# One more expert weight unit in the ring of a hybrid encoder layer, and the memory it moves into

## Chip, core and metric

The kernel runs on one core of a Trainium2 chip. The metric is device time in microseconds of one execution of the whole layer. The profile is of one execution of the same program; its engines are PE (TensorE matmul), PEld (weight load into TensorE), DVE (VectorE), ACT (ScalarE), POOL (GpSimd) and SP (SyncE, which issues nearly all DMAs).

## What is computed

The layer takes 512 tokens of width 1024. Three token mixers (a 2-D neighbourhood attention, a grouped-query attention and a cross-attention into 256 memory tokens) run on one input projection; their outputs are projected, gated, summed and put through an output matrix. Then a layer norm, a router with expert choice (each of 16 experts takes its 64 best tokens), a SwiGLU expert network, and a second layer norm.

```python
merged = jnp.sum(gates * proj, axis=2)
mix = jnp.einsum('bsd,de->bse', merged, w_out[l])
x = layer_norm(DN_ALPHA * x + mix, ln1_g[l], ln1_b[l])
ffn = expert_choice_ffn(x, w_router[l], w_gate_up[l], w_down[l])
x = layer_norm(DN_ALPHA * x + ffn, ln2_g[l], ln2_b[l])
...
h = jnp.einsum('becd,edf->becf', xs, w_gate_up)
hg, hu = jnp.split(h, 2, axis=-1)
ye = jnp.einsum('becf,efd->becd', jax.nn.silu(hg) * hu, w_down)
```

Everything is float32. The experts' weights are 16 times 12 units of 128 partitions x 2048 numbers, which is 1,048,576 bytes a unit: 8 units of gate and up ("gu") and 4 of down ("dn") for each expert. They are 201 of the 251 MB that the kernel moves.

## The kernel before

The order of work is written out by hand; no scheduler moves it. Each engine runs its instructions in program order, and tiles of a pool that share a tag share memory: a later tile of the tag waits until the earlier one has been read for the last time.

Stages, in order: memory tokens and their keys; queries; the gates and projections of the three branches, with attention units interleaved; `g_na_gates` (eight gate products of branch 0); `g_na_proj` (eight projections of branch 0, numbered j = 0 to 7); the output product (`wo`, then `woc` for the second half of the columns) with the first layer norm and the router's logits mixed in; sorting of the affinities to find each expert's cut; then the 16 experts, and the second layer norm.

**Splitting.** Weights of the dense part come by `Stream` (L149 on): a raw unit is loaded (L167), ACT casts its high part (L97) and DVE subtracts to get the low part (L98); a product is three matmuls of high and low parts. The raw buffer has two halves, so a load waits for the DVE of two units before.

**`g_na_proj` (L961 to L980).** For each j: 12 matmuls into a PSUM bank of the tag `mm` (three banks in turn); then on DVE L971 (gate times product, which empties the bank), L972 (add the sum so far); on ACT L973 (the high part `mh`); on DVE L980 (the low part `ml`), one j later. Every second j a unit is split: ACT L97, DVE L98. `run(gen)` (L803 on) takes one background function from the list `bg` after every piece; that is how small work is put between.

**Router preparation (L920 to L950).** `rt` is a tile in the memory tag `bf` that holds small arrays: the scaled router weights `wg_t`, their sums, statistics, counts. `router_scale` (two products and two reductions on DVE, L938 and L939), `router_sums` (one matmul, L943) and `router_centre` (two DVE operations, L946 and L947) are in `bg` while `g_na_gates` runs.

**The ring of expert units.** `RING` names 12 places in memory (tags); ten hold two units, `raw` and `VS` hold one: 22 units in the first round. `_blocks` gives the order in which units of the sequence 0 to 191 go to places: in the first round one DMA brings a whole place; in the second, up to unit 35, one DMA brings one unit. Three places drop out after one or two rounds. `Ring.load` (L822 on) issues one DMA on SP's queue; `Ring.done` is called when the matmuls of a unit have been emitted and issues every load whose place is then free, so each load waits on SP for the PE's last read of that place. The first four places load during `g_na_gates` and `g_na_proj`, two more at the end of the dense units, `Q6` and `raw` by `ring.upto(8)` in the output product, and `Q9`, `VS`, `G1`, `M` (7 units) by `ring.upto(len(RING))` after it, since those hold arrays of the output product until it ends.

**Other homes.** `gb` (15 x 1024) holds the rows of both layer norms; they are loaded early into `ropesq` (L872), cast by ACT (L877) and corrected by two DVE operations (L881, L884). `r_transpose` puts transposed tokens in two buffers of the tag `tmp`; `a01` and `a23`, the arrays that are sorted, are in two buffers of the tag `t`. In the expert part `hT` and `GT` share the two `tmp` buffers and `GTe` takes `bf`.

**An expert (loop at the end of `layer_kernel`).** `gate_up` (L1312) for the first four units, `h_transpose` of the expert before, `down` of the expert before (L1347), then the other four units; `act_h` (ACT L1322, DVE L1323 and L1324); `slots_T` (L1367) for each pair of experts, `combine` for a finished pair, `gather` after every fourth expert (L1272, L1274) and in pieces during the first two.

Of the kernel before, what the change touches and what calls it, by code (L numbers as in the profile page):

```python
# [9 lines left out]
F32 = mybir.dt.float32  # L10
# [30 lines left out]
def lead(e):  # L41
    return 2 if e == NEXP - 2 else 4


def _blocks():
    order = []
    for e in range(NEXP - 1):
        order += [("gu", e, k) for k in range(lead(e))]
        if e:
            order += [("dn", e - 1, k) for k in range(4)]  # L50
        order += [("gu", e, k) for k in range(lead(e), KD)]
    order += [("gu", NEXP - 1, k) for k in range(KD)]
    order += [("dn", e, k) for e in (NEXP - 2, NEXP - 1) for k in range(4)]
    blocks, i, r = [], 0, 0
    while i < len(order):
        for tag, n in RING:
            left = ROUNDS.get(tag, len(order)) - r
            if left > 0 and i < len(order):
                keys = order[i:i + n]
                i += n  # L60
                if r and (i < FULL or i > len(order) - N_SINGLE):
                    blocks += [(tag, h, [key]) for h, key in enumerate(keys)]
                else:
                    blocks.append((tag, 0, keys))
        r += 1
    return blocks
# [3 lines left out]
def layer_kernel(ctx: ExitStack, tc: tile.TileContext, xt, xn, first0, wu, bgate, rpb, gains, wrt,  # L70
# [193 lines left out]
    nc.sync.dma_start(lnT[:, :2], lnt)  # L264
    gb = cp.tile([15, D], F32R, name="gb")
    gb_s, gb_c, gb_t = (cp.tile([15, n], F32, name="gb_" + k)[:, :1] for k, n in (("s", 1), ("c", 1), ("t", 33)))
# [185 lines left out]
    def g_gqa():  # L452
# [23 lines left out]
        a, b = rope[1:]  # L476
        bg.extend([lambda: None, a[4], b[0], a[5], b[1], b[2], b[3], norm_hi, b[4], b[5]])

# [335 lines left out]
    class Ring:  # L814
# [52 lines left out]

    norm_raw = []

    def load_norms():  # L870
        norm_raw.append(vs_t[:15, 1])
        nc.sync.dma_start(norm_raw[0], lnp)  # L872

    after[14] = [load_norms]

    def norm_hi():
        nc.scalar.copy(gb, norm_raw[0])  # L877

    def norm_mask():
        norm_raw.append(vs_t[:15, 0])  # L880
        nc.vector.tensor_scalar(norm_raw[1], gb.bitcast(F32), gb_c, None, op0=ALU.mult)  # L881

    def norm_lo():
        nc.vector.scalar_tensor_tensor(gb, norm_raw[0], gb_s, norm_raw[1], op0=ALU.mult, op1=ALU.add)  # L884


# [32 lines left out]

    rt = R("bf", [P, 12, 64], "rt")  # L920
    aff = rt[:, 0].rearrange("p (m e) -> p m e", m=NT)
    cnt = rt[:, 2:4].rearrange("p a (m e) -> p m a e", m=NT)
    st_all = rt[:, 5:7].rearrange("p a b -> p (a b)")[:, :96].rearrange("p (m q s) -> p m q s", m=NT, q=4)
    ones_f = rt[:, 7:9].rearrange("p a b -> p (a b)")
    nc.gpsimd.memset(ones_f, 1.0)
    lgA = rt[:, 9].rearrange("p (m e) -> p m e", m=NT)
    rb = rt[:, 10][:, :NEXP]
    wsum = rt[:, 10][:, NEXP:3 * NEXP].rearrange("p (a e) -> p a e", a=2)
# [3 lines left out]
    wg_t = rt[:, 2:4].rearrange("p a (k e) -> p (a k) e", e=NEXP)  # L932
    wb_t = rt[:, 0:2].rearrange("p a (k e) -> p (a k) e", e=NEXP)
    wps = []
# [18 lines left out]
    dump("ynh", ST["y0"][0].bitcast(F32))  # L953
    dump("macc", ST["macc"])

# [25 lines left out]

    tri_t = [rt[:, 4].bitcast(F16), rt[:, 11].bitcast(F16), tri_d]
    for i in range(3):
# [12 lines left out]
    a01 = R("t", [48, P], "a01", bufs=2)  # L996
    a23 = R("t", [48, 64 + P], "a23", bufs=2)
    nc.gpsimd.memset(a01, 0.0)
    nc.gpsimd.memset(a23, 0.0)
    top = cp.tile([48, 64], F32, name="top")  # L1000
# [125 lines left out]
    us += ws.take(2)  # L1126
    ring.upto(8)

# [76 lines left out]
    keep_warm(28)  # L1205
    ring.upto(len(RING))
    dump("aff", aff)
# [95 lines left out]
    def gate_up(e, ks):  # L1303
# [3 lines left out]
        for k in ks:  # L1307
            w = ring.get("gu", e, k)
            xs = XS[qd][k // 4][:, k % 4, i * CAP:(i + 1) * CAP]
            for b in range(2):  # L1310
                for hf in range(2):
                    nc.tensor.matmul(GU[e][b][hf * 64:hf * 64 + 64], xs,  # L1312
                                     w[b][:, hf * 512:hf * 512 + 512],
                                     start=(k == 0), stop=(k == KD - 1))
# [11 lines left out]
    def h_transpose(e, tp=None):  # L1326
# [4 lines left out]
        if e == 0:  # L1331
            homes.extend((R("tmp", [P, 4, P], "hT", bufs=2), R("tmp", [P, NT, P], "GT", F32R, bufs=2)))
        t = R("bf", [P, 4, P], f"hT{e}") if e == NEXP - 1 else homes[0]
# [29 lines left out]
    def slots_T(pr):  # L1363
        qd, h = divmod(pr, 2)
        gp = PB("mm", f"gT{pr}", (P, NT, P))
        for m in range(NT):
            nc.tensor.matmul(gp[:, m], OH[qd][:, m, h * P:(h + 1) * P], id16, start=True, stop=True)  # L1367
        if pr == 0:
            homes.append(R("bf", [P, NT, P], "GTe", F32R))
        g = homes[1 if pr % 2 else 2]  # L1370
        GT[pr] = g
# [4 lines left out]
    def acc_of(m):  # L1376
# [3 lines left out]
        return ACC[m // 2][:, m % 2]  # L1380

    def ln_row(row, h, nm):
        bc = PB("mm", nm)
        nc.tensor.matmul(bc, gsel[:, row:row + 1].to_broadcast([15, P]), gb[:, h * 512:h * 512 + 512], start=True, stop=True)
        return bc
# [60 lines left out]
    def last_down(g2, xq, spare):  # L1446
# [118 lines left out]
        def low_rank(m, h):  # L1565
            nc.tensor.matmul(tl[m, h], rows[:13, m * P:(m + 1) * P], gb[:13, h * 512:h * 512 + 512], start=bool(h), stop=True)

# [20 lines left out]
    g1 = gather(0, 2, 2)  # L1588
    side = iter(())
    for e in range(NEXP):  # L1590
        if e == 0:
# [4 lines left out]
        elif e < NEXP - 1:  # L1596
# [207 lines left out]
```

## Time and profile before

| | us |
|---|---|
| median of 3 runs | 966.16 (965.75 to 966.56) |
| the profiled execution, its own time | 966.82 |
| its span in the profile | 965.0 |
| PE busy in it | 942.6 (98%) |
| DVE busy | 453.4 (47%) |
| ACT busy | 276.5 (29%) |
| POOL busy | 84.2 (9%) |

The span is the time between the first and the last instruction, and all places in time below are microseconds from its start. 1.8 us of the profiled execution lie around its span. The granted TensorE clock is 0.997 of full speed over the execution. A matmul's end is modelled, and matmuls overlap, so "PE busy" does not say that PE is at its peak.

### The profile page before, as it was taken

Reading aid. Unit: us, or ns where it says so; the run is one execution under the profiler, and the core shown is the slowest. Engines: PE = TensorE matmul, PEld = TensorE weight load, DVE = VectorE, ACT = ScalarE, POOL = GpSimd, SP = SyncE. Lnnn points to the kernel's source line nnn. Section 1 sums busy time; section 2 is a strip of 40 time slices with the busy share of each in tenths; the row PEclk is TensorE's granted clock in tenths of the full one; section 3 lists DMA queues with packets and bytes.
Section 4 is the critical chain, followed back from the end, with each engine's and each line's share of the span. In section 5 each row is a group of like instructions: output and inputs, shape, how many; then the busy total and the mean of one; then the engine's idle time right before and its main releaser. Section 6 shows DMA issues by size and latency. Waiting matters only on the chain.

```text
span 965.0 us, 12910 instructions
## 1 busy us (share of the span) xinstructions
PE 942.6 (98%) x5262; PEld 608.4 (63%) x5262; DVE 453.4 (47%) x851; ACT 276.5 (29%) x539; POOL 84.2 (9%) x98
## 2 busy tenths in 40 slices
PE   9999999999999999999999999999999999998996
PEld 9899878888888888887885333433344333432344
DVE  6347668874376566237454122653322223231426
ACT  6334454543444454223242111100010000100123
POOL 0002303000112231000023000000000000000003
PEclk9999999999999999999999999999999999999998
DMA  9311111111433322564919999999999999999992
GB/s 361 114 67 67 66 66 44 66 58 54 115 91 106 99 83 87 218 266 192 393 43 387 430 418 431 428 432 429 431 429 431 430 431 431 430 430 432 427 410 91
DMA packets 39192, 251.17 MB, mean 260 GB/s; under 512 B 13007, under 2 KB 13391, under 8 KB 24926
## 3 DMA queue, kind: packets, MB, share of 16 engines
q1 hardware_dynamic: 38414, 249.74, 63.8%
q8 instruction: 41, 0.67, 0.3%
q10 hardware_dynamic: 720, 0.62, 0.2%
q14 instruction: 17, 0.14, 0.0%
HBM read 247.46 MB, written 2.10 MB: 259 GB/s over the span
## 4 chain that ended last, share of the span: by engine, by line
PE 79%; DMA 10%; DVE 6%; ACT 2%; issue 2%; POOL 1%; ACTq 0%; DVEq 0%; POOLq 0%; SPq 0%
DMA w<-in_wx 10%; PE g L1312 10%; PE u L1312 9%; PE y L1347 8%; PE gate L282 4%; PE gate L284 4%; PE gate L283 4%; PE gy L670 2%; PE ga L1272 2%; PE pr L282 2%; PE nqk L284 2%; PE nqk L282 2%; PE nqk L283 2%; PE gt L657 1%; PE pr L283 1%
## 5 line engine op out<-in xcount | busy, mean ns | idle before, releaser
L1312 PE MATMUL g<-w,xs 128*64 128x512 f32 x512 | 135.0, 606 | 2.9 <-DMA w<-in_wx 2.9
L1312 PE MATMUL u<-w,xs 128*64 128x512 f32 x512 | 131.6, 592 | 0.0
L1347 PE MATMUL y<-w,hT 128*64 128x512 f32 x480 | 106.6, 594 | 3.3 <-DMA w<-in_wx 2.6
L98 DVE TENSOR_TENSOR y<-y,y 64x512 fp32r<-64x512 f32 x30 | 20.7, 689 | 134.4 <-ACT y L97 134.4
L1312 PEld LDWEIGHTS u<-w,xs 128*64 128x64 f32 x512 | 36.8, 137 | 73.1 <-issue 72.3
L97 ACT CAST y<-y 64x512 fp32r<-64x512 f32 x30 | 17.4, 580 | 224.8 <-PE y L1347 213.5
L98 DVE TENSOR_TENSOR los<-raw_twin,whi 128x1024 fp32r<-128x1024 f32 x42 | 53.4, 1272 | 58.2 <-ACT whi L97 58.0
L1347 PEld LDWEIGHTS y<-w,hT 128*64 128x64 f32 x480 | 33.8, 137 | 72.0 <-issue 64.7
L284 PE MATMUL gate<-xh,los 128*128 128x512 f32 x192 | 74.8, 390 | 0.0
L1312 PEld LDWEIGHTS g<-w,xs 128*64 128x64 f32 x512 | 30.7, 136 | 53.9 <-issue 44.8
L282 PE MATMUL gate<-xh,whi 128*128 128x512 f32 x144 | 57.2, 397 | 0.0
L283 PE MATMUL gate<-xl,whi 128*128 128x512 f32 x144 | 56.1, 390 | 0.0
L1419 DVE TENSOR_TENSOR acc<-acc,cb 128x512 f32<-128x512 f32 x56 | 35.6, 684 | 37.8 <-PE cb L1417 37.8
L97 ACT CAST whi<-raw_twin 128x1024 fp32r<-128x1024 f32 x42 | 44.0, 1049 | 8.2 <-PE wo L1110 4.3
L1488 POOL TENSOR_TENSOR acc<-acc,ln2g 128x512 f32<-128x512 f32 x6 | 7.6, 1276 | 430.1 <-DVE l2s L1516 428.1
L284 PEld LDWEIGHTS gate<-xh,los 128*128 128x128 f32 x192 | 36.0, 188 | 7.7
L98 DVE TENSOR_TENSOR los<-raw_twin,los 128x1024 fp32r<-128x1024 f32 x20 | 25.0, 1249 | 27.0 <-ACT los L97 26.9
L646 ACT ACTIVATE att_twin<-gs,nm 128x512 f32<-128x512 f32 x32 | 21.7, 684 | 49.0 <-DVE nm L645 49.0
L1322 ACT ACTIVATE tg<-g 128x512 f32<-128x512 f32 x16 | 9.5, 597 | 89.2 <-PE g L1312 89.2
L1335 DVE COPY hT<-ht 128x512 f32<-128x512 f32 x15 | 10.4, 691 | 44.4 <-PE ht L1330 44.4
L282 PEld LDWEIGHTS gate<-xh,whi 128*128 128x128 f32 x144 | 27.0, 188 | 6.5 <-issue 1.2
L283 PEld LDWEIGHTS gate<-xl,whi 128*128 128x128 f32 x144 | 27.1, 188 | 5.3
(436 smaller groups left out, 1863.5 us busy)
## 6 DMA issues: line engine op xcount, KB each, us to landing
w<-in_wx SPq DMA_DIRECT2D x83, 2048.0 KB
raw_twin<-in_wu SPq DMA_DIRECT2D x65, 512.0 KB
w<-in_wx SPq DMA_DIRECT2D x26, 1024.0 KB
raw<-in_wu SPq DMA_DIRECT2D x8, 512.0 KB
xr<-in_xt SPq DMA_DIRECT2D x4, 512.0 KB
macc<-in_xn SPq DMA_DIRECT2D x2, 1024.0 KB
first<-in_first SPq DMA_DIRECT2D x4, 384.0 KB
bf<-in_rpb SPq DMA_DIRECT2D x64, 24.0 KB
```

The costliest lines, as they stand in the source:

```text
L97: nc.scalar.copy(hi, src)
L98: nc.vector.tensor_tensor(lo, src, hi.bitcast(F32), op=ALU.subtract)
L282: nc.tensor.matmul(acc, w_h, rh[:, k], start=(k == 0), stop=False)
L283: nc.tensor.matmul(acc, w_h, rl[:, k], start=False, stop=False)
L284: nc.tensor.matmul(acc, w_l, rh[:, k], start=False, stop=(k == nk - 1))
L646: nc.scalar.activation(self.p[:, h], self.s[h], AF.Exp, bias=nm[:, h:h + 1], accum_out=self.sm[:, h:h + 1])
L670: nc.tensor.matmul(self.y[h * 64:h * 64 + 64, :P], ST["vg"][:, kc, kvh * 64:kvh * 64 + 64], self.pt[:, h, kc], start=(kc == 0), stop=(kc = ...
L1272: nc.tensor.matmul(g, XH[:, m, c], oh[:, m, sl], start=(m == 0), stop=False)
L1312: nc.tensor.matmul(GU[e][b][hf * 64:hf * 64 + 64], xs, w[b][:, hf * 512:hf * 512 + 512], start=(k == 0), stop=(k == KD - 1))
L1335: nc.vector.tensor_copy(t, tp)
L1347: nc.tensor.matmul(y[o * 64:o * 64 + 64], hT[:, c, hf * 64:hf * 64 + 64], w[j][:, o * 512:(o + 1) * 512], start=(k == 0 and j == 0), stop= ...
L1419: nc.vector.tensor_tensor(a, a, cb, op=ALU.add)
```

## The change

A thirteenth entry "X" is put into the first round of the ring, right behind `raw`. It holds unit 22 (expert 2, gate and up, k = 2) and is used once. It lies in three pieces: the up half in the tag `gb` (4 KB a partition), the two quarters of the gate half in `bf` and in one buffer of `tmp` (2 KB each). Three DMAs bring it. So the second round begins with unit 23 in place of 22.

The memory comes from here: the norm rows are no longer kept from the start; `norm_rows` loads them in two halves (15 x 512) during experts 2 and 3 into `gb`, after X is used, with three DVE operations each. The router's arrays leave `bf` for two tiles of the tag `t`, so they are set up after `g_na_gates`, and the `bg` list with `router_scale`, `router_sums` and `router_centre` now runs during `g_na_proj`; the affinities get a tile of their own. The sorted arrays are parts of the second tile. One of the two buffers of the transposed tokens goes to the tag `oh`. `slots_T(0)` moves from expert 1 to expert 2. Empty functions keep the other entries of `bg` where they were.

```diff
 def _blocks():
+        if r == 0:
+            blocks.insert([t for t, _, _ in blocks].index("raw") + 1, ("X", 0, order[i:i + 1]))
+            i += 1
         r += 1
...
 class Ring:  # load
+            if tag == "X":
+                key, = keys
+                g = [R("bf", [P, 512], "wxa"), R("tmp", [P, 512], "wxb", bufs=2)]
+                u = R("gb", [P, D], "wxc")
+                nc.sync.dma_start(u, src[:, 1])
+                nc.sync.dma_start(g[1], src[:, 0, 512:])
+                nc.sync.dma_start(g[0], src[:, 0, :512])
+                self.t[key] = [g, u]
+                self.at[key] = (tag, 0)
+                self.row += P
+                self.n += 1
+                return
...
-    after[14] = [load_norms]
-    def norm_hi():
-        nc.scalar.copy(gb, norm_raw[0])
...
-    bg.extend([norm_mask, norm_lo])
+    bg.extend([lambda: None, lambda: None])
...
-    rt = R("bf", [P, 12, 64], "rt")
-    aff = rt[:, 0].rearrange("p (m e) -> p m e", m=NT)
...
+    run(g_na_gates(), 1.0)
+    at.drain()
...
+    rt, rt1 = (R("t", [P, 8, 64], n, bufs=2) for n in ("rt", "rt1"))
+    aff = cp.tile([P, NT, NEXP], F32, name="aff")
...
+    a01 = rt1[:48, 2:4].rearrange("p a b -> p (a b)")
+    a23 = rt1[:48, 4:7].rearrange("p a b -> p (a b)")
...
     bg.extend([lambda: None, router_scale, lambda: None, router_sums, router_centre])
-    run(g_na_gates(), 1.0)
-    at.drain()
...
+    x1T = [R("tmp", [P, 4, P], "x1T", bufs=2), R("oh", [P, 4, P], "x1To")]
     def r_transpose(m, k0, n=4):
-        t = R("tmp", [P, n, P], f"x1T{m}{k0}", bufs=2)
+        x1T.append(x1T.pop(0))
+        t = x1T[0][:, :n]
...
-    ring.upto(8)
+    ring.upto(9)
...
-    ring.upto(len(RING))
+    ring.upto(len(RING) + 1)
...
+    def norm_rows():
+        GB.append(R("gb", [15, D], "gb", F32R))
+        for h in range(2):
+            c = slice(h * 512, h * 512 + 512)
+            raw = R("t", [15, 512], f"nraw{h}", bufs=2)
+            nc.sync.dma_start(raw, lnp[:, c])
+            yield
+            part = R("t", [15, 512], f"npart{h}", bufs=2)
+            nc.vector.tensor_copy(GB[0][:, c], raw)
+            nc.vector.tensor_scalar(part, GB[0][:, c].bitcast(F32), gb_c, None, op0=ALU.mult)
+            nc.vector.scalar_tensor_tensor(GB[0][:, c], raw, gb_s, part, op0=ALU.mult, op1=ALU.add)
+            yield
...
                 if k == lead(e) - 1:
                     h_transpose(e - 1)
+                    if e in (2, 3):
+                        steps(nrm)
...
-            if e % 2:
-                slots_T(e // 2)
+            if e % 2 and e > 1 or e == 2:
+                slots_T((e - 1) // 2)
...
             for k in range(lead(e), KD):
+                if e in (2, 3) and k == KD - 1:
+                    steps(nrm)
                 gate_up(e, (k,))
```

More of the change, by code (lines that the diff above doesn't have):

```diff
@@ L476, in g_gqa @@
         a, b = rope[1:]
-        bg.extend([lambda: None, a[4], b[0], a[5], b[1], b[2], b[3], norm_hi, b[4], b[5]])
+        bg.extend([lambda: None, a[4], b[0], a[5], b[1], b[2], b[3], lambda: None, b[4], b[5]])
     def g_na_v():
@@ L866, in layer_kernel @@
     vs_t = R("VS", [P, 2, 1024], "ropesq")
[L868 to L872, printed above, removed]
-    after[14] = [load_norms]
-    def norm_hi():
-        nc.scalar.copy(gb, norm_raw[0])
[L879 to L884, printed above, removed]
     run(g_mem())
@@ L918, in layer_kernel @@
     run(g_branch(1, False, between), 0.5)
-    rt = R("bf", [P, 12, 64], "rt")
-    aff = rt[:, 0].rearrange("p (m e) -> p m e", m=NT)
-    cnt = rt[:, 2:4].rearrange("p a (m e) -> p m a e", m=NT)
-    st_all = rt[:, 5:7].rearrange("p a b -> p (a b)")[:, :96].rearrange("p (m q s) -> p m q s", m=NT, q=4)
-    ones_f = rt[:, 7:9].rearrange("p a b -> p (a b)")
-    nc.gpsimd.memset(ones_f, 1.0)
-    lgA = rt[:, 9].rearrange("p (m e) -> p m e", m=NT)
-    rb = rt[:, 10][:, :NEXP]
-    wsum = rt[:, 10][:, NEXP:3 * NEXP].rearrange("p (a e) -> p a e", a=2)
+    run(g_na_gates(), 1.0)
+    at.drain()
+    dump("ynh", ST["y0"][0].bitcast(F32))
+    dump("macc", ST["macc"])
+    rt, rt1 = (R("t", [P, 8, 64], n, bufs=2) for n in ("rt", "rt1"))
+    aff = cp.tile([P, NT, NEXP], F32, name="aff")
+    cnt = rt[:, 0:2].rearrange("p a (m e) -> p m a e", m=NT)
+    st_all = rt[:, 4:6].rearrange("p a b -> p (a b)")[:, :96].rearrange("p (m q s) -> p m q s", m=NT, q=4)
+    ones_f = rt[:, 6:8].rearrange("p a b -> p (a b)")
+    nc.gpsimd.memset(ones_f, 1.0)
+    lgA = rt1[:, 0].rearrange("p (m e) -> p m e", m=NT)
+    rb = rt1[:, 1][:, :NEXP]
+    wsum = rt1[:, 1][:, NEXP:3 * NEXP].rearrange("p (a e) -> p a e", a=2)
+    a01 = rt1[:48, 2:4].rearrange("p a b -> p (a b)")
+    a23 = rt1[:48, 4:7].rearrange("p a b -> p (a b)")
+    nc.gpsimd.memset(a01, 0.0)
+    nc.gpsimd.memset(a23, 0.0)
     tri_d = cp.tile([P, P], F16, name="tri_d")
@@ L931, in layer_kernel @@
     nc.gpsimd.memset(ones_h, 1.0)
-    wg_t = rt[:, 2:4].rearrange("p a (k e) -> p (a k) e", e=NEXP)
-    wb_t = rt[:, 0:2].rearrange("p a (k e) -> p (a k) e", e=NEXP)
+    wg_t = rt[:, 0:2].rearrange("p a (k e) -> p (a k) e", e=NEXP)
+    wb_t = rt[:, 4:6].rearrange("p a (k e) -> p (a k) e", e=NEXP)
     wps = []
@@ L1331, in h_transpose @@
         if e == 0:
-            homes.extend((R("tmp", [P, 4, P], "hT", bufs=2), R("tmp", [P, NT, P], "GT", F32R, bufs=2)))
+            homes.append(R("tmp", [P, 4, P], "hT", bufs=2))
         t = R("bf", [P, 4, P], f"hT{e}") if e == NEXP - 1 else homes[0]
@@ L1367, in slots_T @@
             nc.tensor.matmul(gp[:, m], OH[qd][:, m, h * P:(h + 1) * P], id16, start=True, stop=True)
-        if pr == 0:
-            homes.append(R("bf", [P, NT, P], "GTe", F32R))
-        g = homes[1 if pr % 2 else 2]
+        if pr < 2:
+            homes.append(R("tmp", [P, NT, P], "GT", F32R, bufs=2) if pr else R("bf", [P, NT, P], "GTe", F32R))
+        g = homes[1 + pr % 2]
         GT[pr] = g
@@ L1380, in acc_of @@
         return ACC[m // 2][:, m % 2]
+    GB = []
+    def norm_rows():
[10 more added lines that the diff above has]
+            yield
     def ln_row(row, h, nm):
         bc = PB("mm", nm)
-        nc.tensor.matmul(bc, gsel[:, row:row + 1].to_broadcast([15, P]), gb[:, h * 512:h * 512 + 512], start=True, stop=True)
+        nc.tensor.matmul(bc, gsel[:, row:row + 1].to_broadcast([15, P]), GB[0][:, h * 512:h * 512 + 512], start=True, stop=True)
         return bc
@@ L1565, in low_rank @@
         def low_rank(m, h):
-            nc.tensor.matmul(tl[m, h], rows[:13, m * P:(m + 1) * P], gb[:13, h * 512:h * 512 + 512], start=bool(h), stop=True)
+            nc.tensor.matmul(tl[m, h], rows[:13, m * P:(m + 1) * P], GB[0][:13, h * 512:h * 512 + 512], start=bool(h), stop=True)
         def finish(m, h):
@@ L1589, in layer_kernel @@
     side = iter(())
+    nrm = norm_rows()
     for e in range(NEXP):
```

11 lines of the change are left out of this document (2 added, 9 removed).

## The prediction, made before the changed kernel ran

> **What bounds the kernel now.** I read the page first: the row of transfer rates by slices, since the change concerns transfers.
>
> ```profile
> GB/s 361 114 67 67 66 66 44 66 58 54 115 91 106 99 83 87 218 266 192 393 43 387 430 418 431 428 432 429 431 429 431 430 431 431 430 430 432 427 410 91
> ```
>
> A slice is 24.1 us. From slice 22 to 38, the whole expert part, the rate stands at 427 to 432 GB/s: the queue is full and stays full. Before that lies slice 20 (482 to 506 us) with 43 GB/s, the pause. At 430 GB/s a unit of 1,048,576 bytes takes 2.44 us. Next the chain of waits from its end backwards (start, duration, what), to see whether that rate sets the end:
>
> ```profile
> 842.93 33.97 DMA w<-in_wx
> ...
> 915.86 19.56 DMA w<-in_wx
> ...
> 935.55 1.98 PE yq L1467 x32
> ```
>
> From 843 us to the first of the last four product parts at 935.55 the chain is transfers alone. A transfer issued at 842.93 needs 34 us to land because of those queued before it, so the expert part ends when its bytes have come, plus a fixed tail of PE and DVE work. Then busy time by stretches (PE, PEld, DVE, ACT, POOL, clock, DMA share, GB/s):
>
> ```profile
> 428.00:452.00 24.00, 22.76 (x99) 18.22 (x98) 20.01 (x28) 8.38 (x13) 0.00 (x0) 1.00 0.53 208
> 452.00:503.00 51.00, 50.72 (x294) 43.86 (x294) 25.79 (x67) 15.83 (x30) 3.68 (x14) 1.00 0.54 212
> 484.00:500.00 16.00, 16.00 (x104) 14.30 (x103) 8.66 (x38) 4.36 (x10) 2.94 (x11) 1.00 0.00 1
> 502.00:570.00 68.00, 66.19 (x450) 32.47 (x449) 22.83 (x83) 15.77 (x30) 11.51 (x12) 1.00 0.97 394
> 502.00:574.00 72.00, 70.19 (x468) 33.82 (x469) 23.52 (x84) 15.77 (x30) 11.51 (x12) 1.00 0.97 396
> 502.00:591.00 89.00, 87.19 (x547) 39.42 (x547) 26.34 (x88) 17.53 (x33) 11.51 (x12) 1.00 0.98 403
> 860.00:940.00 80.00, 73.75 (x374) 26.90 (x372) 20.75 (x34) 11.67 (x21) 0.00 (x0) 1.00 1.00 426
> ```
>
> Between 860 and 940 us PE is idle for 6.25 of 80 us: it has caught up with the transfers and waits for them. That 6.25 us is also all that PE can lose in the expert part before it takes over as the bound. The start of the stream is in SP's waits (us in total, times, longest):
>
> ```profile
> SPq L829 <- PE woc L1109: 25.7, 1, 25.7
> ```
>
> SP waits 25.7 us for the output product to let go of `Q9`'s memory, until 502.9. So the stream starts when PE gets there, and between 452 and 503 PE idles 0.28 of 51 us: what makes PE late at 452 makes the stream, and the end, equally late.
>
> **The unit in the pause: -2.44 us.** X stands on SP's queue behind `raw` and before `Q9`. Its memory is free by then (norm rows gone, `bf` last read by the position bias, `tmp` by the last low part). The transfers end at about 483 us and the stretch from 484 to 500 us moved 1 GB/s, so 2.44 us of transfer, and more than that, are covered by 16 idle us. From 502.9 on, the same places are freed by the same PE work as before, each filled by the unit one further on, and the stream is one unit shorter. This counts in full as long as the queue doesn't run dry where the extra unit is spent. In the third filling of `Q2` (units 44 and 45 in place of 43 and 44) the load must wait for unit 24 and no longer 23.
>
> ```profile
> 502.90 65.34 SPq L829 DMA_DIRECT2D w<-in_wx  x21
> ```
>
> and, in the chain of waits:
>
> ```profile
> 572.04 6.87 PE y L1347 x32
> ```
>
> Those 21 loads, issued by 568.2, are 7 units of the first round, 12 single ones and 9 more in five loads, in all 28. Moved by 574 are 72 us x 396 GB/s = 28.5 MB = 27.2 units (the load that followed at 572 stands behind these). Unit 24 is the first quarter of the product at 572.04, done at 573.8; 0.8 unit, 2.0 us of transfer, is then still queued. `slots_T(0)`, gone from expert 1, lets it be some 0.4 us earlier. So the queue is thin there, but not dry. Price if it is: at most the delay itself, 6.87 / 4 = 1.72 us.
>
> By the Trainium skill (DMA: Bandwidth & Descriptors, Specifications) a core's share of HBM is about 358 GB/s, which would make the unit worth an estimated 2.93 us and the sum below 0.49 us better; the rows at 430 GB/s decide against it.
>
> **The router's preparation, moved from the gates to the projections: +1.59 us.** Six DVE operations move. Their rows, four then two:
>
> ```profile
> 391.95 0.28 DVE L938 TENSOR_TENSOR rt<-wr_t,lnT 128x128 f32<-128x128 f32 x1
> ...
> 393.18 1.22 DVE L98 TENSOR_TENSOR los<-raw_twin,los 128x1024 fp32r<-128x1024 f32 x1
> ...
> 405.10 0.17 DVE L946 COPY rt<-wps 128x16 f32<-128x16 f32 x1
> 405.18 0.28 DVE L947 SCALAR_TENSOR_TENSOR rt<-wps,rt 128x128 f32<-128x128 f32 x1
> ```
>
> The four hold DVE from 391.95 to 393.18, 1.23 us; the two from 405.10 to 405.46, 0.36 us. Where they were, DVE waited between splits, so they cost nothing. Where they go, it does not (DVE, then ACT):
>
> ```profile
> 428.19 1.23 DVE L98 TENSOR_TENSOR los<-raw_twin,los 128x1024 fp32r<-128x1024 f32 x1 [6.42 <-ACT los L97]
> 429.34 0.68 DVE L971 SCALAR_TENSOR_TENSOR tm<-sg,pr 128x512 f32<-128x512 f32 x1
> 430.05 0.69 DVE L972 TENSOR_TENSOR tm<-tm,macc 128x512 f32<-128x512 f32 x1
> 430.66 0.68 DVE L971 SCALAR_TENSOR_TENSOR tm<-sg,pr 128x512 f32<-128x512 f32 x1
> 431.37 0.69 DVE L972 TENSOR_TENSOR tm<-tm,macc 128x512 f32<-128x512 f32 x1
> 431.98 0.69 DVE L980 SCALAR_TENSOR_TENSOR ml<-tm,mh 128x512 fp32r<-128x512 f32 x1
> 433.71 1.23 DVE L98 TENSOR_TENSOR los<-raw_twin,whi 128x1024 fp32r<-128x1024 f32 x1 [1.04 <-ACT whi L97]
> ```
>
> ```profile
> 432.10 0.63 ACT L973 ACTIVATE mh<-tm 128x512 fp32r<-128x512 f32 x1 [0.69 <-DVE tm L972]
> 432.64 1.04 ACT L97 CAST whi<-raw_twin 128x1024 fp32r<-128x1024 f32 x1
> ```
>
> DVE's only pause here is 1.04 us, and it is DVE's own doing: the cast it waits for stands on ACT behind the `mh` copy, which waits for L972. So DVE and ACT form one closed chain, 20.01 us of DVE work in 24, and at its end PE waits for it:
>
> ```profile
> PE wo L1108 <- DVE tm L971: 1.2, 2, 0.8
> ```
>
> ```profile
> 450.32 0.50 PE L1108 MATMUL wo<-whi,mh 128*128 128x512 f32 x1 [0.45 <-DVE tm L971]
> ```
>
> `router_scale` now stands ahead of L971 of j = 1, `router_centre` ahead of L971 of j = 4. Both push every later L971, `mh`, cast and split by their whole length; queued behind them are the emptying of a PSUM bank and ACT's casts, and PE waits for the bank of j = 7 at 450.32. That start moves by 1.23 + 0.36 = 1.59 us. `router_sums` takes one of the three `mm` banks between j = 3 and 4, so PE stands earlier (at j = 4 until L971 of j = 2, at j = 6 until `router_centre`), but these stalls end before the chain does. Bounds: 0, if DVE takes the six in its waits; 2.0, with another 0.4 for PE's restarts at the borrowed bank. I take 1.59: each row of the chain starts as the one before it ends.
>
> **The matmul of `router_sums`, out of the gates: -0.22 us.** PE is never idle there, so its place shows in the steps:
>
> ```profile
> 402.10 0.30 PE L943 MATMUL wps<-rt 128*128 128x32 f32 x2
> 402.24 0.48 PE L282 MATMUL gate<-xh,los 128*128 128x512 f32 x1
> 402.55 0.40 PE L283 MATMUL gate<-xl,los 128*128 128x512 f32 x1
> ```
>
> L283 would follow 0.23 us after 402.10; it starts 0.22 us later than that. In `g_na_proj` the matmul falls into PE's new waits.
>
> **The norm rows: +0.14 us.** Two loads of 30 KB inside the full stream, 61 KB at 430 GB/s. Their six DVE operations (an estimated 1.4 us a half, from half of the old row below and its two companions) lie in DVE's waits in experts 2 and 3, at 26.34 us busy of 89. Removing the old cast and two corrections gains nothing: PE has no wait near them.
>
> ```profile
> L884 DVE SCALAR_TENSOR_TENSOR gb<-ropesq,gb_s x1: 1264/1264/1264, 193.2 to 193.2; 15x1024 fp32r<-15x1024 f32 x1
> ```
>
> ```profile
> 606.78 0.60 ACT L1322 ACTIVATE tg<-g 128x512 f32<-128x512 f32 x1 [3.97 <-PE g L1312]
> ```
>
> ```profile
> 502.90 86.68 SPq L829 DMA_DIRECT2D w<-in_wx  x27
> ```
>
> The second half is the delicate one: its DVE operations stand ahead of expert 3's `act_h`, whose ACT step, at 606.78, must wait for them (it reuses the buffer). It is issued behind the 27th load (the last row, one unit later than there), at about 591 us. By then 28 + 6 x 2 = 40 units are issued and 89 x 403 = 35.9 MB, 34.2 units, moved: 5.8 units, 14.1 us, are ahead of it. It lands near 605, is worked off by 607, and PE loses at most some tenths, out of its 6.25 us.
>
> Homes of transposes, sorted arrays, `hT` and `GT`: as many buffers as before, same instructions, nothing.
>
> **Sum:** -2.44 + 1.59 - 0.22 + 0.14 = -0.93 us. On the profiled execution's 966.82 (span 965.0 and 1.8 around it) that is 965.9; it lies 0.66 above the median, so I expect a median of **965.2**.
>
> **The rivals.**
> - *The six operations cost nothing* (bound 0). For: DVE is idle 17% of 428 to 452. Against: the closed chain. 966.16 - 2.44 - 0.22 + 0.14 = 963.6.
> - *The queue runs dry where X is spent.* For: 2.0 us of reserve only. Against: it is positive, and later loads come every 3.4 us for 4.9 us of transfer. 965.2 + 1.72 = 966.9.
> - *The norm rows land late*, and DVE, ACT and then PE stand behind them; PE becomes the bound and the kernel slower. PE can lose 6.25 - 1.37 - 0.93 = 3.95 us, and three free PSUM banks of `gather` give some 2.6 more; so it decides from a landing at about 612. For: the 34 us of the chain's first row; by it the rows land at 625, 13 us past that point: 978. Against: 5.8 units queued, not 14. By the Trainium skill (DMA: Bandwidth & Descriptors, Queues, rings and completion order) an engine takes descriptors in ring order, so nothing lets the small load pass; the 34 us row agrees.
>
> **How the numbers follow.** Chances: forecast 0.58, free operations 0.20, dry queue 0.12, late rows 0.10. About 0.2%, 1.93 us, is what a measurement of this kernel can tell from no change: faster is below 964.23, slower above 968.09. Faster: all of the second case and 0.06 of the forecast's spread, 0.26. Slower: the late rows, 0.02 of the forecast, 0.02 of the dry queue with DVE's upper bound, 0.14. Within: 0.60. The range goes from the free operations (963.6, less 0.3 for a queue better fed in expert 1) to the dry queue plus 0.4 at the banks, 963.3 to 967.4, and leaves out the late rows and edges. The forecast's own is 964.4 to 966.2.
>
> **What would show it.** X's three loads near 478 to 480 us and next to nothing moved from 488 on; the wait of `wo` on L971 ending near 451.7 and the stream's first load near 504.3, both 1.4 late; no rate below 380 GB/s around 574 to 580; the end of the transfers 0.9 earlier than before; PE's waits for them in the last 80 us shrinking from 6.2 to about 4. Wrong it is if `wo` starts on time, if the rate dips at 575, or if ACT waits for DVE at expert 3.

## The result: 967.4 us, a fifth of a per cent slower

| | before | after |
|---|---|---|
| median, 21 runs each, us | 965.84 (965.04 to 968.42) | 967.40 (965.88 to 972.14) |
| ratio, 95% interval | | 1.0021 (1.0014 to 1.0029) |
| executions above 968.5 us | 0 of 21 | 5 of 21, three of them at 972.0 to 972.1 |
| the profiled execution, its span | 966.82, 965.0 | 972.00, 970.2 |

The forecast was 965.2 with a range up to 967.4: wrong in sign, with the median on the range's upper end. The profiled execution of after is one of the three long ones, so a second profile of the same kernel, of an execution of 966.51 us (span 964.7), is read beside it. It is called the repeat.

First the transfer rates by slices (24 us each) of the page, the long execution, then the repeat:

```profile
GB/s 359 112 66 66 66 66 54 56 74 36 127 112 74 95 84 85 261 268 178 394 94 381 429 420 388 372 416 430 431 429 430 431 430 432 430 431 432 427 399 92
```

```profile
GB/s 358 115 67 67 66 66 48 62 68 44 115 116 82 98 83 88 230 278 169 400 78 384 429 426 433 398 418 428 430 432 428 431 431 429 431 431 431 428 406 92
```

Before, slices 23 to 27 stood at 418 to 432 GB/s. The long execution has 388, 372 and 416 in slices 24 to 26, the repeat 398 and 418 in 25 and 26. Elsewhere in the expert part the rates are those of before. Now stretches of the long execution (columns as in the prediction):

```profile
484.00:500.00 16.00, 16.00 (x104) 14.26 (x103) 8.63 (x37) 4.16 (x10) 2.82 (x11) 1.00 0.10 40
502.00:574.00 72.00, 70.19 (x468) 34.03 (x469) 23.71 (x84) 15.37 (x29) 11.49 (x12) 1.00 0.97 398
574.00:600.00 26.00, 26.00 (x126) 8.65 (x122) 5.13 (x8) 2.34 (x4) 0.00 (x0) 1.00 1.01 394
600.00:640.00 40.00, 35.61 (x196) 15.84 (x194) 20.80 (x36) 5.64 (x10) 0.00 (x0) 0.96 1.00 377
640.00:700.00 60.00, 60.00 (x266) 22.50 (x264) 24.86 (x36) 4.10 (x7) 0.00 (x0) 1.00 1.01 431
860.00:940.00 80.00, 74.83 (x340) 25.54 (x336) 21.33 (x34) 10.26 (x18) 0.00 (x0) 1.00 1.01 429
```

and of the repeat:

```profile
574.00:600.00 26.00, 26.00 (x126) 8.53 (x122) 5.13 (x8) 2.34 (x4) 0.00 (x0) 1.00 1.01 430
600.00:640.00 40.00, 38.59 (x216) 16.69 (x216) 25.31 (x40) 6.26 (x11) 0.00 (x0) 1.00 0.98 402
612.00:636.00 24.00, 23.24 (x128) 9.74 (x129) 15.10 (x24) 2.29 (x4) 0.00 (x0) 1.00 0.97 389
```

X's transfer ends by 488 us, in the pause, as meant. After that, 574 to 640 us is where time is lost: against 430 GB/s the long execution loses 26 x (1 - 394/430) + 40 x (1 - 377/430) = 7.1 us, the repeat 40 x (1 - 402/430) = 2.6 us. The long one moves less with its DMA engines just as busy (share 1.00 to 1.01), the repeat with a share of 0.97 to 0.98. That is the first sign of two different losses. The third thing in this stretch is the norm rows' second half, in the chain of waits of the long execution:

```profile
591.60 19.65 DMA nraw<-in_lnp
...
611.27 0.43 DVE gb L1391
...
612.24 0.75 DVE gb L1393
...
613.06 0.04 ACT tg L1321
...
614.16 1.01 PE ga L1271 x4
```

and on ACT in both executions, the long one first:

```profile
613.06 0.60 ACT L1321 ACTIVATE tg<-g 128x512 f32<-128x512 f32 x1 [10.04 <-DVE gb L1393]
```

```profile
609.24 0.60 ACT L1321 ACTIVATE tg<-g 128x512 f32<-128x512 f32 x1 [6.51 <-DVE gb L1393]
```

The load needed 19.65 us (the repeat: 16.1). ACT's step of expert 3 stood at 606.78 before and behind PE; now it stands behind the rows. PE is busy 35.61 and 38.59 of the 40 us, against 39.25 before. The clock of 0.96 in the long execution is one stretch at half the clock, from 614.0 to 617.4 us, which begins at the end of a wait of PE for ACT, 3.64 us long:

```profile
614.00:617.40 3.40, 3.24 (x16) 2.25 (x16) 2.03 (x4) 0.67 (x2) 0.00 (x0) 0.50 0.98 337
```

It adds to PE's delay here, but an execution can be long without it: the long execution with the rows on ACT's queue, below, has a clock of 1.00 throughout these 40 us.

### The profile page after: what moved, and what is told of

Same layout as the page of the kernel before. It is cut to its first block, busy times and chain, and to the rows that moved or that the text cites. A ratio compares the mean times of both kernels' runs of the same rounds, so it can differ in the third digit from the quotient of the medians.

```text
span 970.2 us, 12928 instructions
## 1 busy us (share of the span) xinstructions
PE 944.1 (97%) x5262; PEld 608.8 (63%) x5262; DVE 454.7 (47%) x855; ACT 275.4 (28%) x538; POOL 84.6 (9%) x98
## 4 chain that ended last, share of the span: by engine, by line
PE 80%; DMA 8%; DVE 6%; ACT 2%; issue 2%; POOL 1%; ACTq 0%; DVEq 0%; SPq 0%; POOLq 0%
PE g L1311 10%; PE u L1311 9%; PE y L1346 9%; DMA w<-in_wx 6%; PE gate L284 4%; PE gate L285 4%; PE gate L286 4%; DMA nraw<-in_lnp 2%; PE gy L672 2%; PE ga L1271 2%; PE pr L284 2%; PE cb L1430 2%; PE nqk L285 1%; PE nqk L286 1%; PE nqk L284 1%
```

## Experiments

Medians in us; the ratio is to the kernel before in runs on the same chip, with its 95% interval. The ratio weighs every execution, so long ones lift it above the quotient of the two medians (rows on ACT's queue: 1.0019 against 1.0006). "Above" counts executions above 968.5, which are called long.

| kernel | median (range) | before | ratio | above |
|---|---|---|---|---|
| the changed kernel again | 967.61 (965.82 to 974.11) | 965.91 | 1.0024 (1.0010 to 1.0038) | 3 of 12 |
| rows on ACT's queue | 966.50 (965.22 to 973.53) | 965.91 | 1.0019 (1.0002 to 1.0036) | 4 of 12 |
| no rows | 966.20 (964.97 to 967.09) | 965.91 | 1.0001 (0.9993 to 1.0010) | 0 of 11 |
| no X | 967.31 (966.70 to 971.67) | 965.91 | 1.0023 (1.0013 to 1.0034) | 3 of 11 |
| 16 rows, ACT's queue | 968.27 (965.95 to 971.36) | 965.80 | 1.0021 (1.0009 to 1.0033) | 5 of 11 |
| no rows, single loads | 964.86 (964.29 to 966.37) | 965.80 | 0.9986 (0.9978 to 0.9995) | 0 of 11 |
| 16 rows, single loads | 967.36 (964.31 to 972.32) | 965.80 | 1.0015 (1.0001 to 1.0028) | 2 of 11 |
| 16 rows, single loads, POOL | 967.25 (963.62 to 972.18) | 965.80 | 1.0014 (0.9996 to 1.0032) | 4 of 12 |
| before, single loads | 966.17 (964.31 to 966.96) | 965.64 | 1.0003 (0.9994 to 1.0011) | 0 of 11 |
| rows in expert 4, single loads, POOL | 965.31 (963.66 to 966.74) | 965.64 | 0.9997 (0.9988 to 1.0006) | 0 of 11 |
| rows in expert 4, POOL | 964.44 (963.38 to 967.10) | 965.64 | 0.9987 (0.9978 to 0.9996) | 0 of 11 |
| rows in expert 4 | 966.00 (965.02 to 966.98) | 965.95 | 1.0001 (0.9992 to 1.0010) | 0 of 11 |
| no X, no rows | 966.77 (965.65 to 967.57) | 965.95 | 1.0006 (0.9997 to 1.0015) | 0 of 11 |

### Are late rows the cause, or slower transfers?

The changed kernel again:

> The changed kernel, unaltered, beside a new set of runs of the one before. If the fall of the transfer rate to 383 GB/s between 576 and 640 us and the second half of the norm rows landing at 611 us belong to every execution, both show in this profile and the time is about 967.4, 1.5 above the kernel before. If they belong only to the executions at 972, this profile shows at least 420 GB/s between 576 and 640, ACT waits for DVE at expert 3 for less than 2 us, and the 1.5 us lie somewhere else.

Neither branch came whole: 430 GB/s up to 600 us, then 402, ACT behind DVE for 6.5 us, and a median of 967.61. Then the loads on a queue of their own:

```diff
-            nc.sync.dma_start(raw, lnp[:, c])
+            nc.scalar.dma_start(raw, lnp[:, c])
```

> The two loads of the norm rows are issued by ACT, on a queue of their own, in place of SP. Theory A (late rows: the second half lands some 20 us after its issue because it stands behind the weights, DVE waits for it 6.8 us, ACT 10 us, PE 3.6 us, and loads are freed later): the second half lands within 5 us of its issue, DVE's and ACT's waits are gone and the kernel falls by 2 to 6 us, to 962 to 965.2, below the kernel before. Theory B (the transfers themselves run slower between 576 and 640 us, whatever DVE does): the waits go but the rate stays near 385 to 400 GB/s and the time stays within 0.7 us of the changed kernel, 966.7 to 968.

The second half is issued at 587.3 and its last packet starts at 591.7, and ACT's wait at expert 3 is 3.97 us behind PE, as before the change. By the Trainium skill (DMA: Bandwidth & Descriptors, Queues, rings and completion order) a DMA engine takes turns between the queues that have work for it; 4.4 us here against 16.1 and 19.65 on SP's queue agrees. The common executions fall to 965.2 to 967.3, with a median of 965.94, where the common ones of the changed kernel's second set had 967.45. The 962 to 965.2 of theory A did not come: 4 of 12 are at 968.9 to 973.5, and the profiled one, at 968.9, has the low rate with full DMA engines:

```profile
574.00:600.00 26.00, 26.00 (x126) 8.65 (x122) 5.13 (x8) 2.34 (x4) 0.00 (x0) 1.00 1.01 386
```

So late rows cost some 1.5 us in the common executions, and are not all of it. No rows at all:

```diff
-            nc.sync.dma_start(raw, lnp[:, c])
+            nc.gpsimd.memset(raw, 1.0)
```

> The norm rows are not loaded at all; POOL fills their two buffers with ones and the six DVE operations work on these (the norm rows are left out of the result's second layer norm and residual). Theory A (late rows): as with a queue of their own, 962 to 965.2. Theory B (slower transfers): 966.7 to 968. Should the small packets of the rows (30 of 2 KB) themselves bring the 16 DMA engines out of step and slow the transfers, this kernel alone is back at 430 GB/s between 576 and 640 us and is some 2 to 6 us faster than the one with a queue of their own.

966.20 with no long execution; none of the three expected times. The rows cost 967.61 - 966.20 = 1.4 us at the median, and all of the long executions. But 966.20 is still not below the kernel before, so X's 2.44 us go somewhere else. All moves without X:

```diff
-            blocks.insert([t for t, _, _ in blocks].index("raw") + 1, ("X", 0, order[i:i + 1]))
-            i += 1
...
-    ring.upto(9)
+    ring.upto(8)
```

> All the moves (router preparation in the projections, norm rows in experts 2 and 3, new homes), without the extra unit. By the prediction's terms the moves cost 1.59 - 0.22 + 0.14 = 1.5 us: 967.3 at a kernel before of 965.8. By the trace of the changed kernel, whose stream began only 0.2 us later, they cost 0.3 us plus what late rows do: Theory A then gives 967 to 970 with a stall of ACT at expert 3, theory B (the extra unit upsets the transfers) 966.1 with a rate of 430 GB/s between 576 and 640 us.

967.31, as the prediction's terms have it, though by another sum: the rows' 1.4 are in it, with 3 long executions of 11 and ACT 7.44 us behind DVE. X is therefore not needed for the long executions.

### What the rows do to the transfers

The transfers in 582 to 606 us, long execution and repeat:

```profile
DMA packets 640, 9.37 MB, mean 390 GB/s; under 512 B 68, under 2 KB 68, under 8 KB 68
...
q1 hardware_dynamic: 639, 9.36, 101.2%
```

```profile
DMA packets 734, 10.35 MB, mean 431 GB/s; under 512 B 91, under 2 KB 91, under 8 KB 104
...
q1 hardware_dynamic: 733, 10.33, 100.8%
```

9.36 MB are 571 packets of 16 KB; 16 engines x 24 us x 1.012 / 571 = 0.68 us each. In the repeat it is 0.61. The mean time of the 16 KB packets (ns) by the 5 us in which they start, worked out from the traces' packet records, with some rows left out:

```
from     before  long  repeat  rows on ACT  no X  16 rows  no rows
565         661   621     614          621   635      620      613
570         623   612     611          678   611      711      611
575         611   637     617          681   629      744      633
580         617   677     618          677   618      742      618
590         611   681     611          706   611      709      611
600         611   681     611          681   611      611      611
605         617   694     625          678   652      618      617
610         611   738     611          681   719      611      611
615         613   757     614          642   717      613      637
620         611   697     694          611   615      611      648
625         617   654     669          618   611      617      671
640         611   611     611          611   611      611      611
```

A packet has a normal time, 611 ns, and stretched ones: 681, 720, about 745 and about 758. Where sixteen packets in a row first take 640 ns or more, a half of the norm rows has just passed: its last 2 KB packet starts at 578.1 and the stretch at 578.8 in the long execution, 570.5 and 570.3 with rows on ACT's queue, 570.9 and 571.0 with 16 rows, 608.5 and 608.4 without X (its second half). With 16 rows the stretch ends at 593.5, when the second half has passed (592.7). In the repeat both halves pass without one. So a small load can change the time of all packets behind it, up or down, and does it only in some executions. That the 16 engines are then shifted against each other and get in each other's way is a guess that these records suggest (the packets' starts bunch up); it was not shown. One form of it was tried, that the fault lies with 15 pieces on 16 engines:

```diff
-    r = np.zeros((15, 1024), np.float32)
+    r = np.zeros((16, 1024), np.float32)
...
-            raw = R("t", [15, 512], f"nraw{h}", bufs=2)
-            nc.sync.dma_start(raw, lnp[:, c])
+            raw = R("t", [16, 512], f"nraw{h}", bufs=2)
+            nc.scalar.dma_start(raw, lnp[:, c])
```

> As the kernel with the norm rows on ACT's queue, but the array of rows has a sixteenth row of zeros, so that a load is 16 pieces of 2 KB, one for each DMA engine, in place of 15. Theory C (the 15 pieces put one of the 16 engines out of step, and the 16 KB packets that follow take 681 to 758 ns in place of 611 until the queue thins out): no packets above 640 ns on the mean of any 5 us between 570 and 610 us, no execution above 968.5, median 966.2 as without any rows. Against it (any small load among the large packets can upset them): executions at 969 to 973 remain, about one in four, and the median stays near 966.5.

It fell: 5 long executions of 11, and packets of 740 ns. Over all runs, kernels that load the rows in experts 2 and 3 have 26 of 90 executions above 968.5; those that don't have none of 77, and the kernel before none of 139.

### What became of X's 2.44 us

The last column of the table above has a second kind of entry: 637 to 671 ns at 615 to 630 us, with most packets still at 611. There the queue runs thin. Counting units issued less units moved at each load of the traces (before, and after without rows):

```
load of place    before: issued, units queued    no rows: issued, units queued
M,  3rd          605.92  4.05                    607.52  3.17
Q2, 4th          616.77  1.58                    618.38  0.77
Q1, 4th          621.01  1.84                    623.35  0.91
Q5, 4th          626.16  1.73                    627.76  1.39
```

With X each place holds units that lie one further on, so PE is done with them one unit of work later, and the load that waits for that is issued later, with one unit less behind it. In the gather before expert 4 PE uses no weights for 7.3 us (607.4 to 614.7, without rows), no load is issued from 607.52 to 618.38, and the queue lives on what it has. To give the last units earlier, six of them are loaded one by one:

```diff
-                if r and (i < FULL or i > len(order) - N_SINGLE):
+                if r and (i < FULL or i > len(order) - N_SINGLE or (r == 3 and tag in ("Q2", "Q1", "Q5"))):
```

> The kernel without norm rows (these are left out of the result's residual and second layer norm), and the six units of the fourth filling of Q2, Q1 and Q5 are loaded one at a time, each when its own half is free. Theory D (the queue thins out at the fourth filling of Q2, issued at 618.4 with 0.77 units left, because with X every pair is freed one unit of PE's work later; about 1.5 us of transfer are lost between 612 and 635 us): the first half is issued 1.7 us earlier, the backlog stays above 1 unit, the rate between 600 and 640 us is 425 to 430 GB/s in place of 413 and the time falls by 1.0 to 1.5 us, to 964.7 to 965.2 beside a kernel before of 965.9. If the thin queue is not what X's 2.44 us went to: 966.2, no change.

> Control for theory D: the kernel before (22 units, no X) with the fourth filling of Q2, Q1 and Q5 loaded one unit at a time. It has 1.58 units queued when Q2's fourth load is issued and keeps 430 GB/s, so by theory D the single loads give nothing here: 965.6 to 966.1, as the kernel before. If single loads are better in themselves, whatever X does, it gains 1 us or more: below 965.

Without rows: 964.86 in place of 966.20, as expected, and Q2's fourth filling begins at 616.71 with 1.48 units queued. In the kernel before the same edit gives nothing (1.0003). The stretches of 612 to 636 us, without rows, then without rows and with single loads:

```profile
612.00:636.00 24.00, 23.24 (x124) 9.13 (x124) 15.77 (x24) 2.29 (x4) 0.00 (x0) 1.00 0.99 402
```

```profile
612.00:636.00 24.00, 23.24 (x124) 9.18 (x124) 15.73 (x24) 2.29 (x4) 0.00 (x0) 1.00 1.00 424
```

PE does the same work in both; 402 against 424 GB/s is 24 x 22/430 = 1.2 us, and the medians differ by 1.3. Last, X alone, without rows on either side (the kernel without X fills the buffers of the rows with ones as above):

> All the moves, without X and without norm rows (these are left out of the residual and the second layer norm; POOL writes ones). Against the kernel with X and without rows (966.2 at a kernel before of 965.9) this prices X alone. Theory D (2.44 less some 1.5 to 2 that the thin queue gives back): X is worth 0.4 to 0.9, so 966.6 to 967.1 here. If X were worth its full 2.44 and something else ate it: 968.6. If X is worth nothing: 966.2.

```profile
612.00:636.00 24.00, 23.24 (x126) 9.38 (x125) 15.36 (x24) 2.39 (x5) 0.00 (x0) 1.00 1.01 429
```

Without X no thin queue. 966.77 against 966.20: X is worth about 0.6 us. The two intervals overlap, so the size is uncertain; that a dip of 24 x (429 - 402)/430 = 1.5 us comes with X and goes without it, the two profiles show. Where single loads keep the queue filled, X is worth more: 964.86 (ratio 0.9986, up to 0.9995) with X against 966.77 (1.0006, down to 0.9997) without it, 1.9 us of the 2.44, and these intervals don't overlap. The comparison has single loads on the side with X alone; without X they were run in the kernel before, where they gave nothing.

### The router's preparation, and a version that is faster

```diff
-            nc.vector.tensor_tensor(w, wr_t, lnT[:, i, :, None].to_broadcast([P, KD, NEXP]), op=ALU.mult)
-            nc.vector.tensor_reduce(wsum[:, i], w.rearrange("p k e -> p e k"), axis=AX.X, op=ALU.add)
+            nc.gpsimd.tensor_tensor(w, wr_t, lnT[:, i, :, None].to_broadcast([P, KD, NEXP]), op=ALU.mult)
+            q = rt1[:, 7].rearrange("p (k e) -> p k e", e=NEXP)
+            nc.gpsimd.tensor_tensor(q, w[:, 0:4], w[:, 4:8], op=ALU.add)
+            nc.gpsimd.tensor_tensor(q[:, 0:2], q[:, 0:2], q[:, 2:4], op=ALU.add)
+            nc.gpsimd.tensor_tensor(wsum[:, i], q[:, 0], q[:, 1], op=ALU.add)
```

> Both of these edits together, with the whole result computed: 16 pieces for the norm rows on ACT's queue, and single loads at the fourth filling of Q2, Q1 and Q5. Theories C and D: 964.7 to 965.2. D alone: a fast group at 964 to 965.5 with executions at 968 to 972 beside it. C alone: 966.2.

> As the last, and router_scale's work (its two products, and the two sums as three additions each) is done by POOL, so that four of the six DVE operations, 1.23 us, leave the closed chain of DVE and ACT in the projections. If these operations cost what the prediction said (1.23 us of the start of the output product, and so of the stream and the end), wo starts near 449.3 in place of 450.5, the stream at 501.6 to 501.9 and the time is 1.0 to 1.2 below the kernel with both edits. If DVE's waits have room for them: no change.

Neither expectation came: both medians are spoiled by the rows in experts 2 and 3 (2 and 4 long executions). The starts tell more: with POOL's share, the matmul of `wo` that waits for DVE starts at 449.03 and the stream at 501.56 us, and the fastest executions are at 963.6. So the rows were moved to the thin place, with ACT issuing them in expert 4:

```diff
-            nc.vector.tensor_scalar(part, GB[0][:, c].bitcast(F32), gb_c, None, op0=ALU.mult)
-            nc.vector.scalar_tensor_tensor(GB[0][:, c], raw, gb_s, part, op0=ALU.mult, op1=ALU.add)
+            nc.vector.tensor_scalar(raw, raw, gb_s, None, op0=ALU.mult)
+            nc.vector.scalar_tensor_tensor(GB[0][:, c], GB[0][:, c].bitcast(F32), gb_c, raw, op0=ALU.mult, op1=ALU.add)
...
+                if e == 4 and k == 0:
+                    steps(nrm)
                 if k == lead(e) - 1:
                     h_transpose(e - 1)
-                    if e in (2, 3):
-                        steps(nrm)
+                    if e == 4:
+                        steps(nrm, nrm)
                 gate_up(e, (k,))
-                steps(side, side)
+                if e != 4 or k > 1:
+                    steps(side, side)
```

> X with single loads and with POOL's share of the router, the whole result computed, and the two loads of the norm rows moved to expert 4 (issued by ACT near 615 and 620 us, where the queue holds 1.5 to 2 units; the correction works in place, the residual starts two units later). Theory E (a small load among 16 KB packets can shift the engines against each other, and the packets stay at 681 to 758 ns only as long as the queue is deep; where it is thin or made of 8 KB packets they fall back at once): no executions above 967, median 963.6 to 964.3, 1.7 to 2.2 below the kernel before. If any small load in the stream does the harm: executions at 967 to 972 remain, median near 967 as with rows in experts 2 and 3.

> The same without the single loads. Theories D and E: the queue thins out at the fourth filling of Q2 as in the kernel without rows, so 1.0 to 1.5 us above the one with single loads, 964.8 to 965.5, with no executions above 968, since a queue that runs thin brings the packets back to 611 ns.

> X, the norm rows loaded in expert 4 on ACT's queue, the router's preparation on DVE as in the changed kernel, pair loads. If the four DVE operations of router_scale cost 1.2 us of the stream's start, as the starts of 501.4 to 501.9 us with POOL against 502.8 to 503.1 with DVE say, this one is 1.0 to 1.4 above the version with POOL (964.44): 965.4 to 965.8, the same as the kernel before. If the whole gain came from the rows: 964.4.

No long execution in any of the three. With pair loads and POOL it is 964.44, ratio 0.9987 (0.9978 to 0.9996): faster than both kernels. The rows then cost PE 2.2 us of waits in the residual, where it could spare them (this version, waits: total, times, longest):

```profile
PE r1g L1400 <- DVE gb L1395: 2.2, 2, 1.7
```

Without POOL's share it is 966.00 (a little above what was expected), so those four DVE operations are worth 1.6 us by the medians, 1.3 by the ratios. It also stands level with the kernel without rows (966.20, both ratios 1.0001): in expert 4 the rows cost nothing that these runs can tell. The single loads were expected to give another 1.0 to 1.5 us, and the median with them is 0.9 higher, though the intervals of the two ratios overlap. In its profile their 8 KB packets, 309 ns otherwise, took 329 to 351 from 615 to 630 us, when the rows had passed at 617 and 623. So theory E's packets that fall back at once where they are small did not come.

## Why the prediction was wrong, step by step

**X in the pause, -2.44 us: the step that failed first.** The bytes did move in the pause, and the stream is one unit shorter. What failed is "the same places are freed by the same PE work as before, each filled by the unit one further on". It holds for the first refill alone. From then on a place holds the unit one further on, and so is free one unit of PE's work later. The prediction used this once, for Q2's third filling (0.8 unit left there; nothing ran dry, the rate from 574 us on is 430 in the repeat), and took the question as settled. It comes back at Q2's fourth filling, behind the gather, and that is where 1.5 us are given back. The rival "queue runs dry" had the mechanism and a price of 1.72, but its place 45 us too early. X was worth about 0.6 in place of 2.44, and 1.9 once single loads kept the queue filled. The prediction's opening also misread its own row: it read 427 to 432 GB/s for slices 22 to 38, "the queue is full and stays full", where the row has 418 in slice 23 and 410 in slice 38.

**Norm rows, +0.14 us: the second step that failed.** The sum counted 61 KB at 430 GB/s; the rows measured 1.4 us at the median, and the long executions, 968.6 to 974.1, lie 2 to 8 us above the 966.20 without rows. Two parts of this could be read from before. The landing was put near 605 us and came at 607.4 (repeat) and 611.2; the ACT wait that the prediction named as a sign against it is there. "PE loses some tenths" was near for the repeat (38.59 against 39.24 us busy without rows), but these tenths weren't paid from PE's 6.25 us of spare time at the end: they delay Q2's fourth load from 618.38 to 619.38 us, straight into the thin queue (402 against 413 GB/s from 600 to 640 us, 1.0 us). The stretched packets could not be read from before: no small load stands there in a full stream.

**The router's move, +1.59 us: right, and hidden in the one pair of traces.** The operations stand in the closed chain, end to end, as said (long execution, DVE):

```profile
426.92 1.22 DVE L101 TENSOR_TENSOR los<-raw_twin,los 128x1024 fp32r<-128x1024 f32 x1 [5.91 <-ACT los L100]
428.06 0.68 DVE L971 SCALAR_TENSOR_TENSOR tm<-sg,pr 128x512 f32<-128x512 f32 x1
...
429.38 0.28 DVE L942 TENSOR_TENSOR rt<-wr_t,lnT 128x128 f32<-128x128 f32 x1
...
430.31 0.37 DVE L943 TENSOR_REDUCE rt<-rt 128x16 f32<-128x128 f32 x1
430.60 0.68 DVE L971 SCALAR_TENSOR_TENSOR tm<-sg,pr 128x512 f32<-128x512 f32 x1
...
441.18 0.28 DVE L951 SCALAR_TENSOR_TENSOR rt<-wps,rt 128x128 f32<-128x128 f32 x1
441.38 0.68 DVE L971 SCALAR_TENSOR_TENSOR tm<-sg,pr 128x512 f32<-128x512 f32 x1
```

and yet the waiting matmul of `wo` starts only 0.2 late:

```profile
450.54 0.50 PE L1107 MATMUL wo<-whi,mh 128*128 128x512 f32 x1 [0.47 <-DVE tm L971]
```

The chain itself did grow. From the first L971 to that matmul it took 20.98 us before (429.34 to 450.32) and 22.48 here (428.06 to 450.54). Over all profiles it is 20.98 and 20.99 in the two of the old order, 22.48 to 22.50 in the ten with the preparation on DVE in the projections, and 21.26 to 21.27 in the three with POOL's share. So the six operations cost 1.5 us, and POOL's share takes back 1.23, as their rows said. The rival that they cost nothing is out.

What hid this is that the chain began 1.27 us earlier: the split at 428.19 in the trace of before stands here at 426.92. Of that, 0.5 us is an earlier start of the whole stretch (the split of 386.44 stands at 385.95). The two profiles of the old order differ as much: 386.44, and 385.51 in the kernel before with single loads, the same code up to there. Another 0.28 is the matmul of `router_sums` gone from the gates: the step between the splits at 403.95 and 409.67, 5.7 us in both profiles of the old order, is 5.44 in all the others, where the prediction had 0.22. The last 0.5 lies in the step before the chain, 7.42 and 7.64 us in the old order and 6.94 to 7.46 in the others; why it is shorter is not shown. In all, from the split near 386 us to the waiting matmul it took 63.7 and 63.9 us before and 64.5 to 64.9 with the preparation on DVE, some 0.9 more, and by the medians all moves without X and rows cost 966.77 - 965.95 = 0.8 us (ratio 1.0006, 0.9997 to 1.0015), where the terms had 1.59 - 0.22 = 1.37.

**The sum.** Forecast: 1.37 - 2.44 + 0.14 = -0.9. Measured by medians, each against the kernel before that ran beside it: 0.8 for the moves, -0.5 for X, +1.4 for the rows, together +1.7. These are steps along one row of kernels that ends at the changed kernel's second set of runs, so they must add up to its +1.70; the first set, +1.56, agrees. With the other terms as forecast, either failure alone makes the kernel slower: X at -0.5 gives +1.0, the rows at +1.4 give +0.3. PE's waits in the last 80 us shrank from 6.25 to 5.2 us, not to 4: the transfers' end had hardly moved in the repeat (product parts of the end at 935.49 in place of 935.55).

**The late-rows rival** set its point at a landing of 612 and PE as the bound. The long execution landed at 611.2 and PE did not become the bound; the price came through the transfers.

## What to carry to other kernels

A unit more in a ring moves every later refill by one unit: check the bytes queued at each place where the consumer pauses, in every round, not only where the extra unit is used up. Don't put a small load into a full stream of large ones; put it where the queue is thin, on another queue, and count its long executions as well as its median. A profile of before is one execution: where a step is priced by a start time, look at how far that start varies before the difference of two traces is taken for an effect, or take the time between two points inside the stage.

## What the runs showed of the hardware

16 KB packets of a full queue took 611 ns each; after a load of 15 or 16 pieces of 2 KB had passed, in some executions, nearly all of them took about 680 to 760 ns for 12 us (no X) to 47 us (rows on ACT's queue), and then 611 again, in these traces by 624 us. The DMA engines count as fully busy all the while (share 1.01 at 386 GB/s, rows on ACT's queue). Neither the queue of the small load nor 16 pieces in place of 15 prevents it; what happens in the engines stays open.
